# Last attention unit: P·V in 32-row pieces, with probabilities transposed in place by VectorE

## Chip, cores, metric

The kernel runs on one core of one Trainium2 chip, in one launch. The time is the device time of an execution in microseconds. Before the change it is 1957.69 us, the median of 3 runs (1957.03 to 1958.97).

## What is computed

One layer of a hybrid trunk for a prompt of 1024 tokens and 8 samples of 16 tokens, all in fp32, with weights shared: RMS norm, one large input projection, attention in chunks of 64 frames that see themselves and 8 chunks back, a Mamba-2 scan (SSD) with a causal convolution ahead of it, gates, and an output projection. The change touches only the attention over the prompt, of which this is the core:

```python
def attend(q, k, v, bias, mask):
    s = jnp.einsum('bqhd,bkhd->bhqk', q, k).astype(jnp.float32) * (ATT_HEAD_DIM ** -0.5) + bias[None].astype(jnp.float32)
    s = jnp.where(mask, s, -1e30)
    p = jax.nn.softmax(s, axis=-1).astype(v.dtype)
    return jnp.einsum('bhqk,bkhd->bqhd', p, v)
```

There are 16 heads of 64 channels. The last line, probabilities times V, is what is done in another way, and for the last two heads only.

## The kernel before

**Dense work.** Most of TensorE's time goes to the projections (`dense`, L442, L443, L445; `dense_tok`, L506 to L508): each fp32 product is three fp32r matmuls of 128x128 weights on 384 tokens (high by high, high by low, low by high). The halves of the weights are made by a copy on ScalarE (L334) and a subtraction on VectorE (L335) after a load (L312). A dense result lies in a PSUM bank, `d` (two of them) or `s` (one, shared with the attention scores), until an eviction reads it.

**Attention units.** Eight units, u = 0 to 7, hold two heads each. `prompt()` of a unit goes through 8 blocks of 128 queries, m = 0 to 7, in the four score rounds of the table `ROUNDS` and a last one. A round first transposes the probabilities of the blocks in its third column (`transposed`, L1043: TensorE transposes of 128x128 into a `g` bank, copied back to SBUF on ScalarE at L1045 or VectorE at L1047), then forms P·V of the blocks in its second column (`weigh`, L1066, evicted with the gate at L1127), then the scores of its first column (L1122, into the `s` bank and two `g` banks). After the scores VectorE forms the negated row minimum (`negated`, L1036), ScalarE the exponential (L1031), VectorE the reciprocal and the scale (L1032, L1033). There are four `g` banks. `weigh` uses one of them at a time, the two heads on the two halves of the array's columns: 64 columns of weights each (V) and 128 moving columns. In unit 7 its three calls come to 12, 18 and 30 matmuls of the program, of two passes each, as fp32 takes two.

**What surrounds unit 7.** It is the last attention unit, and its V is ready early: the last token block is projected 45 us before its first P·V. Next comes the SSD part, in head pairs p. Pair 0 first projects its gate `z` (evictions `evz`, L1423 on ScalarE and L1424 on VectorE), then runs its convolution (`conv_gen`: ScalarE L1260, L1265, VectorE L1263 three times, L1269, L1270), and its prelude loads the decay sums `acs_d` to all partitions (L1441) and runs nine ScalarE steps on them (L1453) and an exponential (L1457). The sums come from `dt_gen` (L1291 to L1342). `sample()` (L1152 on) is the samples' attention.

**Order.** A planner on the host runs these parts as generators. It sets their order by a clock of its own (`until`, `pause`, `yield` of a cost), and a scheduler below it places the instructions of each engine by its own estimate, with `late` keeping program order. Each engine then runs its list in order, and waits at the head of it. A generator that finds no slot in SBUF for a buffer is held (`walloc`). The area `varena` (6144 columns) becomes `va_ssd` after unit 7's last token projection (`v_phase("ssd", F32)`), where the layout `L_VT` has five slots `T` of 1184 columns, which `alloc` tries first for the SSD's `T` buffers, `z` among them.

Of the kernel before, what the change touches and what calls it, by code (L numbers as in the profile page):

```python
# [121 lines left out]
def trunk_kernel(ctx: ExitStack, tc: tile.TileContext, h):  # L122
# [41 lines left out]
    def pg(cols=512):  # L164
        return psg.tile([P, 512], F32, tag="g", name=nm("g"))[:, :cols]
# [58 lines left out]
    L_QS = qarena.set_layout(0, [("ada", 1, 1024)])  # L224
    L_VA = varena.set_layout(0, [("ada", 6, 1024)])
    L_VT = varena.set_layout(0, [("T", 5, 1184)])
    v_open = [False]

    def alloc(lay, tag, cols, cold=None):
        if lay is L_Q:  # L230
            try:
                return alloc(L_QR, tag, cols)
            except NoSlot:
                pass
        if lay is L_SSD and tag == "H":
            try:
                return Buf(qarena, qarena.alloc(L_QS, "ada", cols), cols)
            except NoSlot:
                pass
        if lay is L_Q or lay is L_QS:  # L240
            return Buf(qarena, qarena.alloc(lay, tag, cols), cols)
        if lay is L_W3 or lay is L_W7 or lay is L_VT or lay is L_VA:
            return Buf(varena, varena.alloc(lay, tag, cols), cols)
        if lay is L_H or lay is L_W or lay is L_WA or lay is L_QR or lay is L_ST:
            return Buf(rarena, rarena.alloc(lay, tag, cols, cold), cols)
        if (lay is L_SSD or lay is L_HEAD or lay is L_TAIL) and tag == "T" or lay is L_HEAD and tag == "Y":
            if v_open[0]:
                try:
                    return alloc(L_VT, "T", cols)
                except NoSlot:  # L250
                    pass
        return Buf(arena, arena.alloc(lay, tag, cols), cols)
# [659 lines left out]
    def attention(u):  # L912
# [4 lines left out]
        def dense_gen():  # L917
            qk = yield from walloc(lay, "Q", 16 * P)
            v = yield from walloc(lay, big, NT)
            nb = yield from walloc(lay, "n", 84)  # L920
            st["qk"], st["v"], st["nb"] = qk, v, nb
            if u == NU - 1:
                dts["raw"] = yield from walloc(lay, "T", NT)

            def ev(t, ps):

                while t == 8 and "turned" not in st:
                    blocked[0] = "q and k of the first tokens"
                    yield None
                c = qk.ap[:, 2 * (t % 8) * P:2 * (t % 8 + 1) * P]  # L930
                nc.scalar.activation(c, ps[:, :2 * P], AF.Copy)
                s = alloc(lay, "q", 2 * P)
                nc.scalar.activation(s.ap, ps[:, :2 * P], AF.Square)
                nc.vector.tensor_copy(v.ap[:, t * P:(t + 1) * P], ps[:, 2 * P:NQ])
                if u == NU - 1:
                    nc.vector.tensor_copy(dts["raw"].ap[:, t * 32:(t + 1) * 32], ps[:, NQ:])
                nc.vector.tensor_reduce(nb.ap[:, 4 * t:4 * t + 4], s.ap.rearrange("p (h d) -> p h d", d=HD), mybir.AxisListType.X, ALU.add)
                s.free()
                st["n"] = t + 1

            yield from dense_tok(ev)
            dma(h["out_v"][u], v.ap[:, 512:])
            if u == NU - 1:
                v_phase("ssd", F32)
                v_open[0] = True
                return
            z = zs[u + 1] = yield from walloc(lay, "Z" if u + 1 == NU - 1 else "T", NT)
            yield from dense(hops, ev_z(z))
# [72 lines left out]
        def done():  # L1021
            st["left"] -= 1
            att_left[0] -= 1
            if st["left"] == 0:
                dma(att_d[u], st["z"].ap)
                for n in ("z", "v"):
                    st[n].free()
# [21 lines left out]
        def prompt():  # L1049
# [7 lines left out]
            def weigh(js, po):  # L1057
# [16 lines left out]

            ROUNDS = (
# [6 lines left out]
            for pieces, js, ts in ROUNDS:  # L1084
                yield from until(max([sfree[0]] + [tpt[j] for j in js if j in tpt]))
                for m in ts:
                    n = min(m, 4) + 1
                    for e in range(2):
                        yield from until(probs[m] + 700 * e)
                        x, at = place[m][e]  # L1090
                        transposed(x.ap[:, at:at + n * P], x.ap[:, at:at + n * P], n)
                        yield 109 * n
                    tpt[m] = clock[0] + 1500

                yield from until(max([clock[0] + 1000] + [tpt[j] for j in js]) if ts else 0.0)
                cost, po = 0, None
                if js:
                    po = pg(len(js) * P)
                    cost += weigh(js, po)
                for m in sorted({x[0] for x in pieces}):  # L1100
# [21 lines left out]
                            late(nc.tensor.matmul(banks[k][e][:, o:o + w], x.r[hs, qs], y.r[hs, kk], start=i == 0, stop=i == 2))  # L1122
                    cost += 3 * (max(w, 240) / 2.27 + 10)
                yield cost
                if js:
                    ms = slice(js[0] * P, (js[-1] + 1) * P)
                    nc.vector.scalar_tensor_tensor(z.ap[:, ms], po, 0.5, z.ap[:, ms], ALU.mult, ALU.mult)  # L1127
                t = clock[0] + 1000
                for m, c, w, k, o in pieces:
# [8 lines left out]
                    if c + w == n * P:  # L1138
# [7 lines left out]
                        if m == 7:  # L1146
                            for x in st["ops"] + bias:
                                x.free()
                sfree[0] = clock[0] + 300 + sum(3.2 * x[2] for x in pieces)
            done()  # L1150

        def sample():  # L1152
# [772 lines left out]
```

## Time and profile before

| | |
|---|---|
| time, median of 3 runs | 1957.69 us |
| span of the profiled execution | 1955.7 us |
| PE busy | 1938.3 us (99%), 14091 matmuls |
| DVE busy | 1168.5 us (60%) |
| ACT busy | 776.4 us (40%) |
| granted TensorE clock | full in all 40 slices |
| unit 7: scores of the last round on PE | 716.5 to 717.9 us |
| unit 7: last P·V on PE | 735.1 to 738.2 us |

The profiled execution has no time of its own beside its span; the median of the runs stands 2.0 us above that. A group of the profile is a line with an engine, an operation, its tiles and shapes, its count, its busy time, the mean of one instruction in ns, and the idle time before them with what ended it. TensorE's matmuls overlap, so the mean of one (275 ns) is no price; the distance from start to start is. Each matmul has a weight load (PEld) that is counted apart.

### The profile page before, as it was taken

How to read it: one execution, taken by the hardware profiler on the slowest of the kernel's cores; microseconds unless marked ns; L12 is line 12 of the kernel's file. 1: busy time of each engine (PE TensorE's matmuls, PEld its weight loads, DVE VectorE, ACT ScalarE, POOL GpSimd, SP SyncE). 2: the span in 40 equal slices, each digit the busy share in tenths (PEclk: the TensorE clock that was granted, in tenths of full speed). 3: DMA queues.
4: the chain of work that ended last, by engine and by line, in shares of the span. 5: the costliest groups of instructions: out<-in, count | busy, mean ns of one | idle time of the engine just before them, and what ended most of it. 6: DMA issues, size and time to landing. Idle time of an engine off the chain costs nothing.

```text
span 1955.7 us, 35068 instructions
## 1 busy us (share of the span) xinstructions
PE 1938.3 (99%) x14091; PEld 1859.4 (95%) x14091; DVE 1168.5 (60%) x2441; ACT 776.4 (40%) x1589; POOL 323.5 (17%) x624
## 2 busy tenths in 40 slices
PE   7999999999999999999999999999999999999999
PEld 5999999899998999999999999999999999999999
DVE  7455555556555765757566666576674334777732
ACT  8444444445444557344454434345351301111200
POOL 0312213122131201212212221122212100000000
PEclk9999999999999999999999999999999999999999
DMA  9124244232432325433333333332337642331241
GB/s 367 60 81 131 86 132 131 90 122 88 131 112 96 112 88 160 128 112 110 95 132 129 106 103 114 117 118 91 117 118 291 234 140 92 104 104 56 86 143 52
DMA packets 81209, 238.62 MB, mean 122 GB/s; under 512 B 14284, under 2 KB 15320, under 8 KB 81048
## 3 DMA queue, kind: packets, MB, share of 16 engines
q1 hardware_dynamic: 72088, 207.74, 32.7%
q0 software_dynamic: 8960, 28.65, 3.8%
q8 instruction: 111, 1.82, 0.4%
q14 instruction: 50, 0.41, 0.1%
HBM read 192.70 MB, written 43.66 MB: 121 GB/s over the span
## 4 chain that ended last, share of the span: by engine, by line
PE 96%; DVE 1%; ACT 1%; DMA 1%; issue 0%; SPq 0%
PE d L442 13%; PE d L443 13%; PE d L445 13%; PE s L442 5%; PE s L445 5%; PE s L443 5%; PE d L508 5%; PE d L506 5%; PE d L507 5%; PE g L1043 3%; PE g L1066 3%; PE g L1553 2%; PE s L1122 2%; PE g L1526 1%; PE g L1573 1%; PE g L1122 1%
## 5 line engine op out<-in xcount | busy, mean ns | idle before, releaser
L442 PE MATMUL d<-rarena 128*128 128x384 f32 x1520 | 517.4, 340 | 0.3 <-ACT arena L1355 0.3
L445 PE MATMUL d<-rarena 128*128 128x384 f32 x1520 | 511.4, 336 | 0.0
L443 PE MATMUL d<-rarena 128*128 128x384 f32 x1520 | 511.0, 336 | 0.0
L442 PEld LDWEIGHTS d<-rarena 128*128 128x128 f32 x1520 | 285.6, 188 | 4.6 <-issue 2.3
L443 PEld LDWEIGHTS d<-rarena 128*128 128x128 f32 x1520 | 285.6, 188 | 2.8 <-issue 2.4
L445 PEld LDWEIGHTS d<-rarena 128*128 128x128 f32 x1520 | 285.5, 188 | 1.1 <-issue 0.9
L334 ACT ACTIVATE rarena<-arena 128x1024 fp32r<-128x1024 f32 x92 | 97.5, 1060 | 314.1 <-PE s L443 226.2
L442 PE MATMUL s<-rarena 128*128 128x384 f32 x640 | 216.7, 339 | 0.0
L443 PE MATMUL s<-rarena 128*128 128x384 f32 x640 | 214.2, 335 | 0.0
L445 PE MATMUL s<-rarena 128*128 128x384 f32 x640 | 214.1, 334 | 0.0
L508 PE MATMUL d<-va_att,rarena 128*128 128x384 f32 (+1 forms) x559 | 195.0, 349 | 0.0
L506 PE MATMUL d<-va_att,rarena 128*128 128x384 f32 (+1 forms) x559 | 193.9, 347 | 0.0
L507 PE MATMUL d<-va_att,rarena 128*128 128x384 f32 (+1 forms) x559 | 191.0, 342 | 0.0
L335 DVE TENSOR_TENSOR rarena<-arena,rarena 128x1024 fp32r<-128x1024 f32 x92 | 113.2, 1230 | 82.7 <-ACT rarena L334 82.4
L1031 ACT ACTIVATE arena<-arena 128x640 f32<-128x640 f32 (+2 forms) x144 | 101.4, 706 | 138.0 <-DVE arena L1140 99.7
L442 PEld LDWEIGHTS s<-rarena 128*128 128x128 f32 x640 | 120.3, 188 | 1.0 <-issue 1.0
L443 PEld LDWEIGHTS s<-rarena 128*128 128x128 f32 x640 | 120.3, 188 | 0.0
L445 PEld LDWEIGHTS s<-rarena 128*128 128x128 f32 x640 | 120.1, 188 | 0.0
L508 PEld LDWEIGHTS d<-va_att,rarena 128*128 128x128 f32 x559 | 105.5, 189 | 3.9 <-issue 2.7
L1263 DVE SCALAR_TENSOR_TENSOR arena<-arena 128x1176 f32<-128x1176 f32 x66 | 99.9, 1514 | 15.5 <-ACT arena L1260 14.2
L506 PEld LDWEIGHTS d<-va_att,rarena 128*128 128x128 f32 x559 | 105.2, 188 | 3.1 <-issue 1.2
L507 PEld LDWEIGHTS d<-va_att,rarena 128*128 128x128 f32 x559 | 105.2, 188 | 1.0 <-issue 0.4
(345 smaller groups left out, 3212.9 us busy)
## 6 DMA issues: line engine op xcount, KB each, us to landing
arena<-in_wall_dram SPq DMA_DIRECT2D x85, 512.0 KB, 3.9
arena<-in_kc_dram SPq DMA_DIRECT2D x64, 256.0 KB, 4.2
arena<-in_vc_dram SPq DMA_DIRECT2D x64, 256.0 KB, 3.4
arena<-acs_d SPq DMA_DIRECT2D x19, 576.0 KB, 3.8
gate_d<-arena POOLq DMA_DIRECT2D x48, 192.0 KB, 2.5
arena<-y_d SPq DMA_DIRECT2D x15, 576.0 KB, 5.6
arena<-in_wssd_dram SPq DMA_DIRECT2D x16, 512.0 KB, 4.1
arena<-in_wada_dram SPq DMA_DIRECT2D x15, 512.0 KB, 8.9
```

Source lines behind the costliest of these rows:

```text
L334: keep(nc.scalar.activation(hi.r[:, c], b.ap, AF.Copy))
L335: keep(nc.vector.tensor_tensor(lo.r[:, c], b.ap, hi.ap[:, c], ALU.subtract))
L442: nc.tensor.matmul(ps, hi.r[:, wc], kh.r[:, tok], start=k == 0, stop=False)
L443: nc.tensor.matmul(ps, hi.r[:, wc], kl.r[:, tok], start=False, stop=False)
L445: nc.tensor.matmul(ps, lo.r[:, wc], kh.r[:, tok], start=False, stop=k == nk - 1)
L506: nc.tensor.matmul(ps, kh.r[:, tok], wh, start=j == 0, stop=False)
L507: nc.tensor.matmul(ps, kh.r[:, tok], wl, start=False, stop=False)
L508: nc.tensor.matmul(ps, kl.r[:, tok], wh, start=False, stop=j == KT - 1)
L1031: nc.scalar.activation(p, p, AF.Exp, bias=sm_[:, 4 + e:5 + e], scale=-1.0, accum_out=sm_[:, 6 + e:7 + e])
L1043: nc.tensor.transpose(ps[:, s * P:(s + 1) * P], p[:, (j + s) * P:(j + s + 1) * P], ident)
L1122: late(nc.tensor.matmul(banks[k][e][:, o:o + w], x.r[hs, qs], y.r[hs, kk], start=i == 0, stop=i == 2))
L1263: nc.vector.scalar_tensor_tensor(yc, r.ap[:, j:j + n], w4[:, i, j:j + 1], yc, ALU.mult, ALU.add)
```

## The change

For unit 7 alone ("rows" in its state), P·V is cut along the keys into blocks of 32. (1) After V is projected, 16 DMAs copy it inside SBUF into a buffer `vr` of 4096 columns, so that every group of 32 partitions holds all keys' V; `vr` lies in `va_ssd` and is freed when `prompt()` of unit 7 is done. 4096 columns lie over the first four of the five `T` slots. (2) The transposes on TensorE and the copies after them go; `turn` transposes each probability buffer in place on VectorE, in blocks of 32x32 (16 instructions, two for each of the eight m). (3) `weigh_rows` replaces `weigh`. For a block of 32 keys and one or two m it issues 8 matmuls with 32 rows and 64 columns of weights: four row groups (32 queries each), by two column groups (the heads), the moving side 64 or 32 columns. Each row group writes a `g` bank of its own, so it holds all four. Its three calls have 20, 20 and 44 blocks, so 84, or 672 matmuls of the program and 1344 of the profile. (4) Four evictions per call, one for each bank, in place of one. (5) `prompt()` of unit 7 waits for the copies (12 us by the planner's clock), and its P·V now comes ahead of the round's scores with pauses of its own.

```diff
--- before.py
+++ after.py
@@ -224,6 +224,7 @@
     L_QS = qarena.set_layout(0, [("ada", 1, 1024)])
     L_VA = varena.set_layout(0, [("ada", 6, 1024)])
     L_VT = varena.set_layout(0, [("T", 5, 1184)])
+    L_VR = varena.set_layout(0, [("r", 1, 32 * P)])
     v_open = [False]
 
     def alloc(lay, tag, cols, cold=None):
@@ -239,7 +240,7 @@
                 pass
         if lay is L_Q or lay is L_QS:
             return Buf(qarena, qarena.alloc(lay, tag, cols), cols)
-        if lay is L_W3 or lay is L_W7 or lay is L_VT or lay is L_VA:
+        if lay is L_W3 or lay is L_W7 or lay is L_VT or lay is L_VR or lay is L_VA:
             return Buf(varena, varena.alloc(lay, tag, cols), cols)
         if lay is L_H or lay is L_W or lay is L_WA or lay is L_QR or lay is L_ST:
             return Buf(rarena, rarena.alloc(lay, tag, cols, cold), cols)
@@ -942,6 +943,13 @@
             dma(h["out_v"][u], v.ap[:, 512:])
             if u == NU - 1:
                 v_phase("ssd", F32)
+                vr = alloc(L_VR, "r", 32 * P)
+                r4 = vr.ap.rearrange("p (t j c) -> p t j c", j=4, c=P)
+                v3 = v.ap[:, :NP].rearrange("p (t c) -> p t c", c=P)
+                for j in range(4):
+                    for i in range(4):
+                        dma(r4[32 * i:32 * i + 32, :, j], v3[32 * j:32 * j + 32])
+                st["rows"] = vr, clock[0] + 12000
                 v_open[0] = True
                 return
             z = zs[u + 1] = yield from walloc(lay, "Z" if u + 1 == NU - 1 else "T", NT)
@@ -1074,6 +1082,56 @@
 
 
 
+            def turn(m, e):
+                n = min(m, 4) + 1
+                x, at = place[m][e]
+                nc.vector.transpose(x.ap[:, at:at + n * P], x.ap[:, at:at + n * P])
+
+            def weigh_rows(js):
+
+                vr = st["rows"][0].ap
+                pq = [pg(32 * len(js)) for _ in range(4)]
+                first_kb = lambda m: 4 * max(m - 4, 0)
+                ops = []
+                for a in range(0, len(js), 2):
+                    ms = js[a:a + 2]
+                    common = range(first_kb(ms[-1]), 4 * ms[0] + 4)
+                    ops += [(kb, a, ms) for kb in common]
+                    if len(ms) == 2:
+                        ops += [(kb, a, ms[:1]) for kb in range(first_kb(ms[0]), first_kb(ms[1]))]
+                        ops += [(kb, a + 1, ms[1:]) for kb in range(4 * ms[0] + 4, 4 * ms[1] + 4)]
+                begun, left = set(), {a: sum(o[1] <= a < o[1] + len(o[2]) for o in ops) for a in range(len(js))}
+                for kb, a, ms in ops:
+                    begin = a not in begun
+                    for i in range(len(ms)):
+                        assert begin == (a + i not in begun)
+                        begun.add(a + i)
+                        left[a + i] -= 1
+                    end = left[a] == 0 or left[a + len(ms) - 1] == 0
+                    for i in range(4):
+                        rw = slice(32 * i, 32 * i + 32)
+                        for e in range(2):
+                            at = [place[m][e][0].at + place[m][e][1] + 32 * (kb - first_kb(m)) for m in ms]
+                            if len(at) == 1:
+                                mv = arena.base[rw, at[0]:at[0] + 32]
+                            else:
+                                d = at[1] - at[0]
+                                lo = min(at)
+                                mv = arena.base[rw, lo:lo + 2 * abs(d)].rearrange("p (a c) -> p a c", a=2)[:, :, :32]
+                                if d < 0:
+                                    mv = mv[:, ::-1]
+                            he = slice(64 * e, 64 * e + 64)
+                            out = pq[i][he, 32 * a:32 * (a + len(ms))]
+                            if len(ms) > 1:
+                                out = out.rearrange("p (a c) -> p a c", c=32)
+                            late(nc.tensor.matmul(out, vr[rw, kb * P + 64 * e:kb * P + 64 * e + 64], mv, start=begin, stop=end,
+                                                  skip_group_check=True))
+                for j in js:
+                    for x, _ in place.pop(j):
+                        if not any(x is y for q in place.values() for y, _ in q):
+                            x.free()
+                return pq, len(ops) * 16 * 6.7
+
             ROUNDS = (
                 (((0, 0, 128, 0, 0), (2, 0, 384, 0, 128), (1, 0, 256, 1, 0), (3, 0, 256, 1, 256)), (), ()),
                 (((3, 256, 256, 0, 0), (4, 0, 256, 0, 256), (4, 256, 384, 1, 0), (5, 0, 128, 1, 384)), (), (0, 1, 2)),
@@ -1088,13 +1146,24 @@
                     for e in range(2):
                         yield from until(probs[m] + 700 * e)
                         x, at = place[m][e]
+                        if "rows" in st:
+                            turn(m, e)
+                            continue
                         transposed(x.ap[:, at:at + n * P], x.ap[:, at:at + n * P], n)
                         yield 109 * n
                     tpt[m] = clock[0] + 1500
 
                 yield from until(max([clock[0] + 1000] + [tpt[j] for j in js]) if ts else 0.0)
                 cost, po = 0, None
-                if js:
+                if js and "rows" in st:
+                    yield from until(max([st["rows"][1]] + [clock[0] + 2500] if ts else [0.0]))
+                    pq, c = weigh_rows(js)
+                    yield c
+                    zv = z.ap[:, js[0] * P:(js[-1] + 1) * P].rearrange("p (a q c) -> p q a c", q=4, c=32)
+                    for i in range(4):
+                        nc.vector.scalar_tensor_tensor(zv[:, i], pq[i].rearrange("p (a c) -> p a c", c=32), 0.5, zv[:, i], ALU.mult, ALU.mult)
+                    yield from pause(1500)
+                elif js:
                     po = pg(len(js) * P)
                     cost += weigh(js, po)
                 for m in sorted({x[0] for x in pieces}):
@@ -1122,7 +1191,7 @@
                             late(nc.tensor.matmul(banks[k][e][:, o:o + w], x.r[hs, qs], y.r[hs, kk], start=i == 0, stop=i == 2))
                     cost += 3 * (max(w, 240) / 2.27 + 10)
                 yield cost
-                if js:
+                if js and po is not None:
                     ms = slice(js[0] * P, (js[-1] + 1) * P)
                     nc.vector.scalar_tensor_tensor(z.ap[:, ms], po, 0.5, z.ap[:, ms], ALU.mult, ALU.mult)
                 t = clock[0] + 1000
@@ -1147,6 +1216,8 @@
                             for x in st["ops"] + bias:
                                 x.free()
                 sfree[0] = clock[0] + 300 + sum(3.2 * x[2] for x in pieces)
+            if "rows" in st:
+                st["rows"][0].free()
             done()
 
         def sample():
```

How the lists of the engines change shows at three places. Names: `s_`, `g_`, `d_` with a number are PSUM buffers, numbered in the planner's order; line numbers after the change are those of the changed kernel.

TensorE before, at the end of the last round's scores (`g_7549`, `g_7550` are the score banks; `d_7788` and `d_7869` are projections, the first of them `z` of the first SSD pair):

```order
L1122 MATMUL g_7549<-rarena 128x256
L1122 MATMUL g_7550<-rarena 128x256
L1327 MATMUL g_7607<-va_ssd,arena 128x256
L443 MATMUL d_7788<-rarena 128x384
L1335 MATMUL g_7613<-arena 32x128 x4
L445 MATMUL d_7788<-rarena 128x384
L442 MATMUL d_7869<-rarena 128x384
```

Seventy-four more projection matmuls stand between these scores and the last P·V, with the transposes of blocks 6 and 7 among them. The same place after the change (`g_7906` is the first of the four banks of the last P·V, `s_8374` the third part of `z`):

```order
L1191 MATMUL g_7862<-rarena 128x256
L1191 MATMUL g_7863<-rarena 128x256
L1127 MATMUL g_7906<-arena,va_ssd 64x64
L443 MATMUL s_8374<-rarena 128x384
L444 MATMUL s_8374<-rarena 128x384
```

The first matmul of the last P·V now follows the scores directly, then come 24 projection matmuls into the `s` bank, and then the rest of P·V. The earlier P·V calls moved as well: counted in projection matmuls, from 662 after a fixed point to 648 (first call) and from 716 to 696 (second), where the last scores went from 718 to 696.

TensorE before, at the end of the last P·V:

```order
L445 MATMUL s_7947<-rarena 128x384
L1066 MATMUL g_7728<-arena 64x128 x30
L1335 MATMUL g_7777<-arena 32x128
L1202 MATMUL g_7798<-arena 32x128 x20
L442 MATMUL d_7977<-rarena 128x384
```

After the change (`g_7906` to `g_7909` are its four banks):

```order
L1127 MATMUL g_7906<-arena,va_ssd 64x32 x2
L1127 MATMUL g_7907<-arena,va_ssd 64x32 x2
L1127 MATMUL g_7908<-arena,va_ssd 64x32 x2
L1127 MATMUL g_7909<-arena,va_ssd 64x32 x2
L443 MATMUL d_8437<-rarena 128x384
```

`d_8437` is the next projection. All of `z` (`d_8267`, `d_8311`, `s_8374`) now stands ahead of the end of P·V, and it fills both `d` banks and the `s` bank.

ScalarE before, around its last exponentials of unit 7 (L1031), where `z` was evicted already (`d_7788`):

```order
L1423 ACTIVATE va_ssd<-d_7788 128x384
L1336 ACTIVATE va_ssd<-g_7624 32x512
L1045 ACTIVATE arena<-g_7639 128x512
L1031 ACTIVATE arena<-arena 128x640 x2
L1045 ACTIVATE arena<-g_7658 128x512
L1240 ACTIVATE arena<-d_7869 128x384
```

After the change (L1039 is that exponential, L335 the weights' copy, L1524 and L1528 the prelude's steps, L1331 the convolution, L1494 the evictions of `z`):

```order
L1039 ACTIVATE arena<-arena 128x640 x2
L335 ACTIVATE rarena<-arena 128x1024
L1524 ACTIVATE arena<-arena 128x128 x9
L1528 ACTIVATE arena<-arena 128x1152
L1331 ACTIVATE va_ssd<-arena 128x1176
L1494 ACTIVATE va_ssd<-d_8267 128x384
L1336 ACTIVATE arena<-va_ssd 128x1176
L1494 ACTIVATE va_ssd<-d_8311 128x384
L1494 ACTIVATE va_ssd<-s_8374 128x384
```

The evictions of `z` come behind the prelude's nine steps, which need the load of `acs_d`, and behind a convolution step. On VectorE the second half of the eviction of `d_8267` (L1495) comes behind two of that convolution's steps (L1334). On SP's queue the load of `acs_d` (L1512) stands behind two loads of weights (L313), which wait for VectorE's halves (L336).

## Prediction

> **What bounds the kernel now.** I read the head of the page first, then what TensorE waited for.
>
> ```profile
> span 1955.7 us, 35068 instructions
> PE 1938.3 (99%) x14091; PEld 1859.4 (95%) x14091; DVE 1168.5 (60%) x2441; ACT 776.4 (40%) x1589; POOL 323.5 (17%) x624
> ```
>
> ```profile
> PE g L577 <- DMA arena<-in_xT_dram: 8.7, 1, 8.7
> ...
> PE g L1481 <- DVE arena L1269: 1.8, 2, 1.4
> ...
> PE g L1043 <- DVE arena L1036: 0.4, 2, 0.3
> ```
>
> TensorE is busy 99% of the span, and of its idle time 8.7 us are the start. So a microsecond of matmuls saved is a microsecond gained, no wait of VectorE or ScalarE costs anything today, and each wait that the change opens on TensorE costs in full. That leaves two questions: how many microseconds of matmuls go or come, and whether the projections still cover the chain scores, softmax, P·V.
>
> **The matmuls that go and come.** First the groups, then the timeline and the chain for what one instruction really takes (start to start, not its mean).
>
> ```profile
> L1043 PE MATMUL g<-arena 128*128 128x128 f32 x560 | 86.2, 274 | 0.4 <-DVE arena L1036 0.4
> L1066 PE MATMUL g<-arena 128*64 128x128 f32 x960 | 57.7, 275 | 0.0
> ```
>
> ```profile
> 691.72 1.58 PE L1043 MATMUL g<-arena 128*128 128x128 f32 x13
> 693.06 0.42 PE L445 MATMUL d<-rarena 128*128 128x384 f32 x1
> ```
>
> ```profile
> 735.18 3.43 PE g L1066 x60
> ...
> 903.72 0.89 PE g L1560 x32
> ```
>
> 13 transposes run from 691.72 to the next start at 693.06, 0.103 us each; 60 go, 6.2 us. P·V takes 3.43/60 = 0.057 us for each instruction; unit 7's 60 matmuls are 120 instructions, 6.9 us. Added are 84 blocks of 8 matmuls in two passes, 1344 instructions. The nearest row is L1560: 64 columns of weights and 16 moving, two column groups side by side: 0.89/32 = 0.028 us for each, so 0.056 us for a pass of one group. If all eight tiles of a block (four row groups, two column groups) run side by side as these two do, a block is two passes, 0.112 us, and 84 blocks are 9.4 us. If the row groups follow one another, a block is 0.45 us and the sum 37.6 us. For which of the two, the timeline has rows. The first is an answer for a window of 0.027 us:
>
> ```profile
> 657.02 0.32 PE L1202 MATMUL g<-arena 128*32 128x128 f32 x4
> ```
>
> ```profile
> 689.81 0.33 PE L442 MATMUL d<-rarena 128*128 128x384 f32 x1
> 689.98 0.33 PE L443 MATMUL d<-rarena 128*128 128x384 f32 x1
> ...
> 717.49 0.28 PE L1122 MATMUL g<-rarena 64*128 64x256 f32 x2
> 717.60 0.28 PE L1122 MATMUL g<-qa_att,rarena 64*128 64x256 f32 x2
> ```
>
> Four column groups start within 0.027 us, and the two row groups of the scores take 0.11 us a pair with 256 columns, where one projection with 384 takes 0.17, so 256 would take 0.115: a pair costs what one does. Column groups and row groups each run side by side here; that all eight do is an inference. I take 9.4 us, with 37.6 as the upper end; the matmuls then change by 9.4 - 6.2 - 6.9 = -3.7 us.
>
> The Trainium skill ("TensorE: Matmul & The Clock Gate", section "Wait — 56ns, not 53.3ns?") says that matmuls never start closer together than about 25 ns, however few columns move. By it the estimate would be 1344 x 25 ns = 33.6 us in place of 9.4. The four starts within 27 ns speak against it for tiles side by side, but the average of 28 ns over 32 doesn't; it is part of rival one.
>
> **The copies** of V (16 DMAs) have the 45 us between V and its first use, with SP nearly empty: nothing, or a late first P·V.
>
> **The waits that come.** The order shows the new chain: `z` fills both `d` banks and the `s` bank ahead of the last P·V and can't be evicted, so TensorE has no projection to put beside the softmax. Durations:
>
> ```profile
> L335 DVE TENSOR_TENSOR rarena<-arena,rarena 128x1024 fp32r<-128x1024 f32 x92 | 113.2, 1230 | 82.7 <-ACT rarena L334 82.4
> L1263 DVE SCALAR_TENSOR_TENSOR arena<-arena 128x1176 f32<-128x1176 f32 x66 | 99.9, 1514 | 15.5 <-ACT arena L1260 14.2 <-POOL arena L1252 0.7
> L1033 DVE TENSOR_SCALAR arena<-arena 128x640 f32<-128x640 f32 x80 | 51.7, 648 | 2.7
> L1535 DVE SCALAR_TENSOR_TENSOR arena<-arena,g 128x64 f32<-128x64 f32 x224 | 45.9, 274 | 57.4 <-ACT arena L1531 53.1 <-PE g L1526 4.3
> ...
> L1032 DVE RECIPROCAL arena<-arena 128x1 f32<-128x1 f32 x144 | 23.1, 161 | 44.6 <-ACT arena L1031 42.8
> ...
> L1036 DVE CUSTOM_DVE_ANT_0 arena<-s,arena 128x640 f32<-128x640 f32 x16 | 13.1, 821 | 3.7 <-PE s L1178 3.7
> ...
> L1424 DVE SCALAR_TENSOR_TENSOR va_ssd<-va_ssd,d 128x384 f32<-128x384 f32 x21 | 11.5, 546 | 2.5 <-ACT va_ssd L1423 2.5
> ...
> L1036 DVE CUSTOM_DVE_ANT_0 arena<-s,arena 128x512 f32<-128x512 f32 x16 | 10.4, 688 | 2.3 <-PE s L1122 2.3
> ```
>
> ```profile
> L1031 ACT ACTIVATE arena<-arena 128x640 f32<-128x640 f32 x80 | 65.9, 824 | 119.0 <-DVE arena L1140 95.5 <-DVE arena L1036 23.5
> ...
> L1260 ACT ACTIVATE arena<-arena 128x1176 f32<-128x1176 f32 x22 | 30.1, 1370 | 0.6 <-DVE arena L1270 0.2
> ...
> L1031 ACT ACTIVATION_READ_ACCUMULATOR arena<-arena 128x1 f32 x144 | 27.2, 189 | 0.0
> ...
> L1457 ACT ACTIVATE arena<-arena 128x1152 f32<-128x1152 f32 x19 | 22.0, 1160 | 0.2
> ```
>
> ```profile
> 717.69 0.29 DVE L1036 CUSTOM_DVE_ANT_0 arena<-s,arena 128x128 f32<-128x128 f32 x1 [0.79 <-PE s L1122]
> ...
> 718.24 0.16 DVE L1140 TENSOR_TENSOR arena<-arena 128x2 f32<-128x2 f32 x1
> ...
> 722.44 0.42 DVE L1036 CUSTOM_DVE_ANT_0 arena<-g,arena 128x256 f32<-128x256 f32 x1
> ...
> 722.78 0.42 DVE L1036 CUSTOM_DVE_ANT_0 arena<-g,arena 128x256 f32<-128x256 f32 x1
> ```
>
> The last two start 0.34 us apart for a duration of 0.42: in a row, VectorE's instructions cost 0.08 less than they last, and so I count them. The in-place transpose of 640 columns has no row; between the plain pass (0.65) and the pass with a minimum (0.82) I take 0.7. In place of 4 of TensorE's transposes and two copies it now stands on VectorE itself, in the chain.
>
> A, the second P·V needs all four `g` banks. From the end of the first P·V VectorE has to do 4 evictions (0.8), the samples' minimum (0.7), wait for their exponential (0.82 + 0.19), reciprocal and scale (0.7): 3.3 us. ScalarE's convolution step ends at 4.0, the three L1263 at 8.3, two minima of 512 at 9.5, L1140 and the exponential at 10.7, reciprocals and a scale at 11.6, the transpose at 12.3, a scale at 12.9, and the two minima that free the `g` banks at 14.1. TensorE in this time has 31 projection matmuls at 0.173 (5.4), 0.5 of L1335's transposes, and the scores:
>
> ```profile
> 698.06 0.50 PE L1122 MATMUL s<-rarena 64*128 64x512 f32 x2
> ...
> 699.66 0.44 PE L445 MATMUL d<-rarena 128*128 128x384 f32 x1
> ```
>
> 1.6 us, in all 7.5. A is 6.6 us.
>
> B, the first matmul of the last P·V stands directly behind the scores and needs the transposed block 6. From VectorE's first minimum (before, 0.24 us ahead of the scores' end): minima 0.55, L1140, exponential, reciprocal, scale, reciprocal to 2.6, transpose to 3.3: TensorE waits 3.1. `s_8374` needs the `s` bank read: a scale and two minima of 384, 1.4 more. B is 4.5 us. Its 24 matmuls last to 9.0, and the remaining 44 blocks, whose transposes are ready in time (the last at 11.6), to 13.9.
>
> C, `d_8437` needs a `d` bank, so the eviction of `d_8267`.
>
> ```profile
> 762.08 2.74 ACT va_ssd L1453 x9
> ...
> 769.83 4.62 DMA arena<-acs_d
> ```
>
> VectorE finishes the weights' half (L335) at 13.0, behind which SP issues the load of `acs_d`: landed at 17.7. ScalarE's nine steps end at 20.4, the exponential at 21.6, the convolution step at 22.9; two L1263 on VectorE end at 25.8, and L1424 at 26.3. C is 26.3 - 13.9 = 12.4 us. At least it is 1 us (the eviction alone), if the load lands early.
>
> D, the work behind `d_8437` waits for the other evictions, 0 to 2 us: 1.
>
> The waits come to 24.5 us, with 11 to 28 as bounds. Of the waits before, L1043's 0.4 goes and L1481's 1.8 may: -1.
>
> **The clock after a wait.** Two windows at the start, for L577 alone (time busy and count on PE, then on PEld):
>
> ```profile
> 9.67:13.94 4.27, 4.27 (x6) 1.60 (x5) 1.00 1.02 420
> 15.05:17.20 2.15, 2.15 (x6) 0.95 (x5) 1.00 0.98 330
> ```
>
> Five loaded weights, so five matmuls, take 4.27 us after the first idle time and 2.15 us later, twice as fast, though the granted clock reads 1.00 in both. From 8.7 to about 14.4 us TensorE ran at half speed, which loses some 2.7 us. Waits as long as A and C may each bring that back: 0 to 5.4 us; I take 4, since A is the shorter.
>
> By the Trainium skill ("TensorE: Matmul & The Clock Gate", section "What's actually happening") an idle window of about 3.4 us halves the clock until a busy one of the same length, an estimate of 1.7 us lost for each of A and C, 3.4 in place of 4. The start agrees in kind; no longer wait stands in this trace.
>
> The sum: -3.7 + 24.5 - 1 + 4 = +23.8 us, against the span 1955.7, so 1979.5. The runs' median stands 2.0 above the span (1957.69), so 1981.5 us.
>
> **Rivals.** One: the eight tiles don't run side by side, or no instruction comes closer than 28 ns on average; both give 37.6 us in place of 9.4, +28.2. The last P·V then ends at 9.0 + 19.7 = 28.7, behind C's chain, so C falls to 1, and its half-speed stretch goes: 23.8 + 28.2 - 11.4 - 2 = +38.6, 1996 us (by the skill's 25 ns about 1992). For it: no row has eight tiles at once. Against it: rows for both kinds of group.
>
> Two, the other side: TensorE doesn't wait, because the projections cover the chain as they did before, and only the matmuls count: -3.7 - 0.4, 1953.6 us. Its place is the stretch from the first P·V to `d_8437`; it decides once the waits together are under 4 us. For it: 24 of `z`'s matmuls do move into the softmax of block 7, and VectorE is busy 60%. Against it: A needs the 14.1 us chain of VectorE to shrink to 8, and the three banks are held.
>
> Three: the load of `acs_d` lands early, A and B shrink by half, no half speed: 5.5 + 1 + 1 - 4.7 = +3, 1960.5 us.
>
> **How the numbers follow.** The forecast has 0.72, with a range of its own of 1968 (C at 6, clock 0, smaller A) to 1991 (clock 5.4, D 2, a block at 0.2 us, which adds 7.4); rival one 0.13, two 0.09, three 0.06. A measurement of this kernel tells 0.2% (3.9 us) from no change. Faster by more: rival two, 0.09. Within: rival three, 0.06. Slower: 0.85. The range of 8 in 10 reaches down to 1965, leaving out rivals two and three, and up to 1997, to take in rival one.
>
> **What would show it.** Right: TensorE waits of about 6.6 us before the second P·V, 3 and 1.4 around the last one's first matmul, and 12 before `d_8437`, named after VectorE's minima, the transpose and the eviction; 84 blocks in about 10 us outside the waits; half-speed projections for some us behind the long waits. Wrong: blocks of 0.4 us (rival one); TensorE busy 99% with `z` evicted before the prelude's steps (two); the load of `acs_d` landed before the last P·V ends (three).

## The result, and the profile after

The changed kernel takes 1994.45 us, the median of 4 runs (1992.66 to 1996.03), against 1957.36: a ratio of 1.0188, 95% interval 1.0176 to 1.02. It was forecast slower at 1981.5, within 1965 to 1997. The loss is 37 us where 24 were expected, and of another make.

The head of the page after, and the queue that brings the engines their instructions:

```profile
span 1992.8 us, 37402 instructions
PE 1954.8 (98%) x15255; PEld 1872.1 (94%) x15255; DVE 1174.2 (59%) x2456; ACT 767.9 (39%) x1571; POOL 325.6 (16%) x624
...
q8 instruction: 120, 1.97, 0.4%
```

The same queue before:

```profile
q8 instruction: 111, 1.82, 0.4%
```

The span grew by 37.1 us, TensorE's busy time by 16.5 and its idle time by 20.6. What it waited for after the change, in the view of waits (total, times, longest):

```profile
PE g L1127 <- issue: 14.0, 8, 2.2
...
PE g L1127 <- DVE arena L1044: 3.3, 1, 3.3
PE g L1127 <- DVE arena L1088: 3.0, 1, 3.0
...
PE s L443 <- DVE arena L1044: 0.9, 1, 0.9
PE g L1127 <- ACT va_ssd L1407: 0.5, 1, 0.5
```

Four of these lines were forecast: A is 3.3 + 0.5, B is 3.0 + 0.9. The largest was not. "issue" is time in which the engine waited for nothing that the profile shows, and all of it lies inside P·V (L1127). TensorE's timeline shows where:

```profile
741.89 2.26 PE L1127 MATMUL g<-arena,va_ssd 32*64 32x64 f32 x188
746.35 1.73 PE L1127 MATMUL g<-arena,va_ssd 32*64 32x64 f32 x128 [2.20 <-issue]
750.08 2.06 PE L1127 MATMUL g<-arena,va_ssd 32*64 32x32 f32 x128 [2.00 <-issue]
753.81 2.03 PE L1127 MATMUL g<-arena,va_ssd 32*64 32x32 f32 x128 [1.67 <-issue]
757.26 2.04 PE L1127 MATMUL g<-arena,va_ssd 32*64 32x32 f32 x128 [1.42 <-issue]
761.01 0.32 PE L1127 MATMUL g<-arena,va_ssd 32*64 32x32 f32 x2 [1.70 <-issue]
761.25 0.69 PE L443 MATMUL d<-rarena 128*128 128x384 f32 x1
```

Behind the first stretch of 188 matmuls, P·V comes in portions of exactly 128, each with its weight load, so 256 instructions, with a gap behind each. From one portion's start to the next are 3.73 us twice (746.35, 750.08, 753.81), then 3.45 and 3.75; over the four that is 3.67, or 29 ns a matmul. The changed kernel has 15255 - 14091 = 1164 more matmuls, 2328 instructions with their loads, or 9.1 portions of 256, and the instruction queue carried 120 - 111 = 9 more packets, of 16 KB each (1.97 MB / 120). So a portion is one packet of instructions. The trace has the packets' own times, and they agree: between 741.8 and 761.5 us there are 5 packets for the 5 gaps above. They end at 745.09, 748.74, 752.54, 755.88 and 759.47, each 1.3 to 1.5 us before a portion starts, and from the second on each begins 1.0 to 1.2 us after the portion before it has started. So in these rows the next portion hangs on the packet before it, and the packet on the start of the portion before that.

TensorE's time can be added up by line, from each matmul's start to the next one's. P·V in pieces takes 39.6 us, with the gaps and with the 3.3 and 0.9 us of waits that lie inside it. P·V in the old way takes 7.0 us less than before and the transposes 6.5 less. The projections take 4.9 us more, the scores 3.8 more (B's 3.0 among them), the samples' scores 1.5 more. That makes 36.3 of the 37.1.

Apart from the waits of A and B, the projections and scores are dearer because of the clock. Windows of the changed kernel (PE busy and count, then the granted clock):

```profile
700.00:705.00 5.00, 2.89 (x297) 1.00 0.02 3
705.00:710.00 5.00, 5.00 (x47) 0.66 0.02 3
...
720.00:725.00 5.00, 3.59 (x239) 0.50 0.03 7
735.00:740.00 5.00, 5.00 (x16) 0.50 0.30 105
765.00:770.00 5.00, 5.00 (x49) 1.00 0.59 147
```

Between 735 and 740 us 16 projection matmuls take 0.31 us each in place of 0.17. The mean granted clock is 0.989 over the span, which makes 44 us at half clock, all in this stretch.

### The profile page after: what moved, and what is told of

The parts are those of the page before. It is cut to its first block, busy times and chain, and to the rows that moved or that the text cites. A ratio compares the mean times of both kernels' runs of the same rounds, so it can differ in the third digit from the quotient of the medians.

```text
span 1992.8 us, 37402 instructions
## 1 busy us (share of the span) xinstructions
PE 1954.8 (98%) x15255; PEld 1872.1 (94%) x15255; DVE 1174.2 (59%) x2456; ACT 767.9 (39%) x1571; POOL 325.6 (16%) x624
## 3 DMA queue, kind: packets, MB, share of 16 engines
q8 instruction: 120, 1.97, 0.4%
## 4 chain that ended last, share of the span: by engine, by line
PE 94%; DVE 2%; DMA 2%; ACT 1%; issue 1%; SPq 0%; DVEq 0%; ACTq 0%
PE d L443 13%; PE d L444 13%; PE d L446 13%; PE s L443 5%; PE s L444 5%; PE s L446 5%; PE d L509 5%; PE d L507 5%; PE d L508 5%; PE g L1051 3%; PE g L1074 2%; PE g L1624 2%; PE s L1191 2%; PE g L1597 1%; PE g L1191 1%; PE g L1644 1%
## 5 line engine op out<-in xcount | busy, mean ns | idle before, releaser
L443 PE MATMUL s<-rarena 128*128 128x384 f32 x648 | 220.8, 341 | 0.9 <-DVE arena L1044 0.9
L335 ACT ACTIVATE rarena<-arena 128x1024 fp32r<-128x1024 f32 x93 | 98.4, 1058 | 312.9 <-PE s L444 227.2
L444 PE MATMUL s<-rarena 128*128 128x384 f32 x648 | 218.1, 337 | 0.0
L446 PE MATMUL s<-rarena 128*128 128x384 f32 x648 | 217.8, 336 | 0.0
L1039 ACT ACTIVATE arena<-arena 128x640 f32<-128x640 f32 (+2 forms) x144 | 101.5, 706 | 165.9 <-DVE arena L1209 119.4
L336 DVE TENSOR_TENSOR rarena<-arena,rarena 128x1024 fp32r<-128x1024 f32 x93 | 114.2, 1228 | 63.7 <-ACT rarena L335 63.4
L443 PEld LDWEIGHTS s<-rarena 128*128 128x128 f32 x648 | 122.6, 189 | 2.1 <-DVE arena L1044 1.0
L444 PEld LDWEIGHTS s<-rarena 128*128 128x128 f32 x648 | 122.7, 189 | 0.2 <-issue 0.2
L446 PEld LDWEIGHTS s<-rarena 128*128 128x128 f32 x648 | 122.5, 189 | 0.0
L1334 DVE SCALAR_TENSOR_TENSOR arena<-arena 128x1176 f32<-128x1176 f32 x69 | 106.4, 1542 | 16.1 <-ACT arena L1331 15.2
```

Source lines behind the costliest of these rows:

```text
L335: keep(nc.scalar.activation(hi.r[:, c], b.ap, AF.Copy))
L336: keep(nc.vector.tensor_tensor(lo.r[:, c], b.ap, hi.ap[:, c], ALU.subtract))
L443: nc.tensor.matmul(ps, hi.r[:, wc], kh.r[:, tok], start=k == 0, stop=False)
L444: nc.tensor.matmul(ps, hi.r[:, wc], kl.r[:, tok], start=False, stop=False)
L446: nc.tensor.matmul(ps, lo.r[:, wc], kh.r[:, tok], start=False, stop=k == nk - 1)
L1039: nc.scalar.activation(p, p, AF.Exp, bias=sm_[:, 4 + e:5 + e], scale=-1.0, accum_out=sm_[:, 6 + e:7 + e])
```

## Experiments

Two theories after the result. **S (supply):** TensorE's instructions arrive no faster than 256 in 3.7 us, so P·V costs what its number of instructions costs, whatever the array does with them. **R (array):** a block takes the array its time, and the gaps are a fixed cost. Beside them stands the prediction's own reason for the waits, **H (held slots)**, against **O**, that the turn on VectorE moves P·V ahead of the projections.

**Parts of the change alone.** The copies of V with their slots, without turn and pieces:

```diff
-                        if "rows" in st:
+                        if False:
                             turn(m, e)
...
-                if js and "rows" in st:
+                if js and False:
```

> V is copied to the row groups and the copies hold their place among the T slots until unit 7 is done, but the transposes on TensorE and the old P.V stay, so the output is the reference's. Theory H (held slots, the prediction's reason for the waits): z has no slot, projections are missing beside the softmax, and waits of 8 us or more come: 1965 to 1977 us. Theory O (order: the waits come with the turn on VectorE, which costs TensorE nothing, so that P.V moves ahead of the projections): the old order stands, 74 or more projection matmuls remain between the last scores and the last P.V, 1957 us within 4.

1954.4 us (10 runs), ratio 0.9986 (0.9976 to 0.9995): as O has it, and slightly faster than before (0.14%). Its complete list of waits on TensorE:

```profile
PE g L578 <- DMA arena<-in_xT_dram: 7.8, 1, 7.8
PE s L666 <- ACT rarena L647: 0.9, 1, 0.9
PE s L666 <- DVE rarena L659: 0.9, 1, 0.9
PE d L694 <- DVE arena L685: 0.4, 1, 0.4
PE g L1552 <- DVE va_ssd L1340: 0.2, 1, 0.2
```

Of the 1.8 + 0.4 + 0.3 us that TensorE waited before in the middle of the kernel, 0.2 is left, which is most of the 2.8 us gained. With the next run it is the fastest kernel of this study; nobody reads the copies in it, so the gain must be one of order.

The turn alone:

```diff
-                vr = alloc(L_VR, "r", 32 * P)
...
-                        if "rows" in st:
+                        if u == NU - 1:
                             turn(m, e)
```

> The probabilities are turned on VectorE in 32x32 blocks, with no copies of V and no held slots, and the old P.V of 128 rows reads them (a block transpose is not the transpose, so the attention of unit 7 is wrong). Theory H: only the transposes go, 6.5 us, and nothing waits: 1951 us. Theory O: 6.5 us go, waits of 3 to 8 us before the second and the last P.V come, and some us at half clock after them: 1957 to 1964 us.

1954.75 us, ratio 0.9988 (0.9979 to 0.9997): between the two. TensorE waits in three new places, 2.5 + 0.9 + 0.7 us, and the transposes' 6.5 us pay for it. Of the 74 projection matmuls between the last scores and the last P·V 19 are left: the turn does move P·V ahead, as O has it.

Turn and copies, with the old P·V:

```diff
-                if js and "rows" in st:
+                if js and False:
```

> Turn on VectorE and copies of V with their held slots, but the old P.V of 128 rows (unit 7's attention is wrong). Theory H: 8 us or more above the run with the turn alone. Theory O: within 3 us of that run, and the changed kernel stands some 30 us above this one, all of it from the P.V in 32-row pieces.

1960.05 us, ratio 1.0012 (1.0002 to 1.0021), 5.3 above the turn alone: neither 3 nor 8. One wait makes most of it, on the timeline:

```profile
718.02 0.48 PE L1051 MATMUL g<-arena 128*128 128x128 f32 x1 [7.09 <-ACT arena L1053]
```

So without the pieces the change costs about 3 us (0.4 to 4.1 by the interval). The pieces cost 1994.45 - 1960.05 = 34.4 us. Neither theory has the 5.3 us: held slots alone cost nothing (the first run), but beside the turn they do, though nobody reads the copies here. How, these runs don't show.

**What the pieces cost.** Four row groups made one, the blocks kept:

```diff
-                    for i in range(4):
-                        rw = slice(32 * i, 32 * i + 32)
+                    for i in range(4) if begin or end else (kb % 4,):
+                        rw = slice(32 * i, 32 * i + 32) if begin or end else slice(0, P)
```

> The changed kernel, but in all blocks except the first and the last of an output one matmul of 128 rows stands in place of the four of 32 (so P.V sums over the wrong rows): 246 matmuls of the program in place of 672, 492 instructions in place of 1344, with the same 84 blocks, columns, banks and order. Theory S (supply: TensorE's instructions arrive at about 29 ns a matmul once they follow each other so closely, 128 in a burst and then a gap): 852 x 0.029 = 25 us less, 1970 us, and less than that by some us if the clock stays up; the gaps of 1.4 to 2.2 us are gone. Theory R (the array takes 0.16 to 0.25 us for a block, whatever it is made of): only the 14 us of gaps go, 1980 us or more.

1982.0 us, ratio 1.0125 (1.011 to 1.014). By the time alone that is R's range. But the gaps are gone, and P·V without its waits falls from 35.4 to 16.2 us, 19 us less, where R allows 14 and S wants 25. That the time falls by 12.5 only has another reason, to be seen in TensorE's rows:

```profile
733.20 6.21 PE L1127 MATMUL g<-arena,va_ssd 32*64 32x64 f32 x234
...
745.42 1.33 PE L1051 MATMUL g<-arena 128*128 128x128 f32 x5 [6.01 <-DVE arena L1164]
747.73 0.69 PE L443 MATMUL d<-rarena 128*128 128x384 f32 x1 [0.98 <-DVE va_ssd L1495]
```

With P·V over at 739.4, the evictions of `z` and of P·V are late: 7 us of waits come back that the slow P·V had hidden.

Each matmul of P·V twice:

```diff
-                            late(nc.tensor.matmul(out, ..., start=begin, stop=end, skip_group_check=True))
+                            for again in range(2):
+                                late(nc.tensor.matmul(out, ..., start=begin and again == 0, stop=end and again == 1, ...))
```

> The changed kernel with each of the 672 matmuls of P.V issued twice in a row, 1344 more instructions (so its sums are doubled). Theory S (supply): 1344 x 0.029 = 39 us more, 2033 us, with the gaps after each 128 matmuls more than doubled in number. Theory R (the array's own time, 10 to 15 ns a matmul inside a burst, and a fixed number of waits): 13 to 20 us more, 2008 to 2014 us.

2031.3 us (2 runs), ratio 1.0378 (1.0357 to 1.0399): 36.8 us more, S. The portions:

```profile
777.76 2.76 PE L1128 MATMUL g<-arena,va_ssd 32*64 32x32 f32 x128 [1.00 <-issue]
781.49 2.73 PE L1128 MATMUL g<-arena,va_ssd 32*64 32x32 f32 x128 [0.97 <-issue]
785.22 2.73 PE L1128 MATMUL g<-arena,va_ssd 32*64 32x32 f32 x128 [1.00 <-issue]
```

A portion is busy for 2.7 us here and 2.0 in the changed kernel, the gap is 1.0 and not 1.4 to 2.0, and the distance is 3.73 again. Most distances of the two runs lie near it, all between 3.45 and 4.56. It is the distance that stays, and not the gap.

Twice the moving columns:

```diff
-                pq = [pg(32 * len(js)) for _ in range(4)]
+                pq = [pg(64 * len(js)) for _ in range(4)]
...
+                            mv = mv.unsqueeze(1).to_broadcast([32, 2] + list(mv.shape[1:]))
```

> The changed kernel with each matmul's moving columns taken twice (128 or 64 in place of 64 or 32, the second half into columns that nobody reads): the same 1344 instructions, twice the array's moving time. Theory S: the array's time hides in the gaps of the supply, 1994.5 us within 4. Theory R: 168 passes become 0.05 us longer at full clock and 0.1 at half, 8 to 17 us more, 2003 to 2011 us.

1993.0 us, ratio 1.0183 (1.0168 to 1.0199): S; the array's added time went into the gaps (11.4 us of them in place of 14.0), and P·V without its waits takes 36.2 us against 35.4.

One head in most blocks:

```diff
                         for e in range(2):
+                            if e and not (begin or end):
+                                continue
```

> The changed kernel without the second head's matmuls, except in the first and last block of an output (so the second head's P.V is mostly left out): 776 instructions in place of 1344, the same blocks, banks and order. Theory S: 568 x 0.029 = 16.5 us less, of which up to 6 come back as a wait behind the last P.V (as where four row groups were made one): 1978 to 1984 us. Theory R: the two heads stand side by side in the array, so a block takes as long without one; only gaps in proportion go, 14 x 0.42 = 6 us: 1988 us or more.

1983.0 us, ratio 1.0134 (1.0117 to 1.015): in S's range. Where P·V ended, the forecast's wait C stands:

```profile
742.62 2.02 PE L1129 MATMUL g<-arena,va_ssd 32*64 32x32 f32 x74 [2.14 <-issue]
750.47 0.69 PE L443 MATMUL d<-rarena 128*128 128x384 f32 x1 [5.83 <-DVE va_ssd L1497]
```

The pieces with TensorE's transposes:

```diff
-                        if "rows" in st:
+                        if False:
                             turn(m, e)
```

> The changed kernel, but with the transposes on TensorE as before (so P.V in 32-row pieces reads wrongly ordered probabilities). The order has no projections between the last scores and the last P.V here either. Theory: the pieces carry nearly the whole loss, and the turn on VectorE saves them 60 transposes and shortens the chain: 6.5 us and 2 to 6 us of waits more than the changed kernel, 2003 to 2007 us. Rival: the turn is what makes the pieces dear (it fills VectorE and takes the projections away): then this run lies 10 us or more below the changed kernel, 1984 us or less.

1994.6 us, ratio 1.0191 (1.0176 to 1.0206), the changed kernel's time. Neither side of the expectation: the turn doesn't make the pieces dear, but it doesn't save them 6.5 us either. By line, the transposes take 10.7 us more than in the changed kernel, waits of 3.0 us included, P·V 4.4 less, since A and B are not there, and the projections 5.2 less. The slots are held in this kernel, so held slots and pieces without the turn don't make A and B.

**Held slots and the place of the instructions.** No copies, V read where it lies:

```diff
-                vr = alloc(L_VR, "r", 32 * P)
...
-                st["rows"] = vr, clock[0] + 12000
+                st["rows"] = v, clock[0] + 12000
...
-    vr[rw, kb * P + 64 * e:kb * P + 64 * e + 64]
+    vr[rw, kb // 4 * P + 64 * e:kb // 4 * P + 64 * e + 64]
```

> The changed kernel without the copies: the pieces read V where it lies (so keys and V don't belong together), nothing lies in z's slots, and no eviction of z waits for the last P.V. In the runs with copies but without pieces nobody read the copies, so z's evictions had nothing to wait for, and held slots were not tried there. Theory H (held slots take the projections away): the order has 94 projection matmuls between the last scores' start and the last P.V again; the waits before the second and the last P.V go (3.3 + 0.5 + 3.0 + 0.9 us) and some 3 us of projections at half clock with them: 1984 us. Rival: the waits belong to the turn or to the four banks: 1994 us within 3.

1981.0 us, ratio 1.0129 (1.0113 to 1.0144): H, by 3 us more than expected. In TensorE's list of waits A and B are gone, and in P·V only the supply is left:

```profile
PE g L1121 <- issue: 12.4, 7, 2.2
```

The same kernel with projections between the blocks (a lock keeps the planner's other parts out meanwhile):

```diff
+                    if len(done_) % 2:
+                        yield 214
+                        yield from pause(200)
...
-                    pq, c = weigh_rows(js)
+                    lock[0] = cur[0]
+                    pq, c = yield from weigh_rows(js)
```

> The run without the copies, with P.V in the same 1344 instructions but three projection matmuls after every second block. Theory S (supply): two blocks and three projections are 70 instructions in about 1.06 us, so 256 in 3.9 us, about what the supply gives; the gaps go, a block costs 0.27 us (0.15 for its passes, the rest for changing between tiles and the whole array), 84 of them 23 us in place of 35: 1967 us. Rival: P.V costs what its instructions take wherever they stand, and each change adds: 1984 us or more.

1976.4 us, ratio 1.0103 (1.0088 to 1.0118): between the two, 4.6 below the run before it. Two blocks and what stands around them:

```profile
745.43 0.49 PE L1126 MATMUL g<-arena 32*64 32x64 f32 x32
745.85 0.44 PE L443 MATMUL d<-rarena 128*128 128x384 f32 x1
746.13 0.34 PE L444 MATMUL d<-rarena 128*128 128x384 f32 x1
746.30 0.33 PE L446 MATMUL d<-rarena 128*128 128x384 f32 x1
746.57 0.49 PE L1126 MATMUL g<-arena 32*64 32x64 f32 x32
```

For P·V S has it: no gaps between these blocks, 32 matmuls in 0.42 us to the next projection, and P·V's whole time down from 31.6 to 21.7 us (some of it still stands in two long portions, with 4.0 us of gaps). What was not expected is the price around it: three projections take 0.72 us from 745.85 to 746.57 in place of 0.52, so each change to the tiles and back costs 0.2. Only the last P·V call came out spread, with 22 such changes, 4.4 us in all; the projections take 4.1 us more than in the run before.

No copies, and one matmul of 128 rows for four of 32:

```diff
-                    for i in range(4):
-                        rw = slice(32 * i, 32 * i + 32)
+                    for i in range(4) if begin or end else (kb % 4,):
+                        rw = slice(32 * i, 32 * i + 32) if begin or end else slice(0, P)
...
-                st["rows"] = vr, clock[0] + 12000
+                st["rows"] = v, clock[0] + 12000
```

> The run without the copies, with one matmul of 128 rows in place of four of 32 in all blocks but the first and the last of an output (P.V sums over the wrong rows), 492 instructions. Theory: with neither held slots nor more instructions than the supply gives, what is left is 1957.4 - 13.5 for the matmuls removed + 492 x 0.025 = 12.3, 1956 us. Rival: the waits behind P.V that this kernel with the copies showed (6 us) stay: 1962 us or more.

1965.5 us, ratio 1.0049 (1.0032 to 1.0066): 9 above the theory and in the rival's range, but not with the rival's 6 us of waits. P·V took 14.4 us against the 13.5 saved, so the pieces would not have gained even at 492 instructions. In the profiled execution, with a span of 1960.2, a wait of 3.3 us stands behind P·V; what the other runs spent beyond that is open.

## The prediction, step by step

- **What bounds it: right.** With TensorE at 99%, every added matmul and wait was paid.
- **Matmuls removed:** 13.1 us forecast, 13.5 measured.
- **Blocks: the step that failed.** "84 blocks are 9.4 us" became 39.6 less the waits inside (4.2), 35.4 us. That tiles run side by side was right: in the spread run the eight matmuls of a pass start within 0.05 us, and 32 take 0.42 us to the next projection, 13 ns each; the fastest portion of the changed kernel is through in 1.73 us, 13.5 ns a matmul. But a rate per instruction from a run of 32 says nothing of 1344: behind the first portion they come at 29 ns. Rival one named this number ("no instruction comes closer than 28 ns on average"), with its time, 1996, and 0.13; it is the case that came, by another mechanism than tiles one after another.
- **A:** 6.6 forecast, 3.8 measured. VectorE's chain was right: 14.1 us forecast, 13.8 measured from its first eviction at 705.24 to TensorE's start at 719.03. TensorE had 10.0 us to do meanwhile and not 7.5, mostly since its projections ran at half clock for some of it.
- **B:** 4.5 forecast, 3.9 measured, at the place and behind the instructions named.
- **C:** 12.4 forecast, none measured. Its chain came as written, only later, and P·V was slower still. On VectorE and ScalarE after the change:

```profile
730.08 0.29 DVE L1044 CUSTOM_DVE_ANT_0 arena<-s,arena 128x128 f32<-128x128 f32 x1 [1.45 <-PE s L1191]
...
756.34 2.92 DVE L1334 SCALAR_TENSOR_TENSOR va_ssd<-arena,va_ssd 128x1176 f32<-128x1176 f32 x2 [4.68 <-ACT va_ssd L1331]
759.18 0.55 DVE L1495 SCALAR_TENSOR_TENSOR va_ssd<-va_ssd,d 128x384 f32<-128x384 f32 x1
```

```profile
751.12 2.74 ACT L1524 ACTIVATE arena<-arena 128x128 f32<-128x128 f32 x9 [8.23 <-DMA arena<-acs_d]
```

  The eviction ends 29.6 us after VectorE's first minimum (26.3 forecast), when P·V, due at 13.9, still has until 31. Rival one had C fall to 1. Where P·V was shortened, C came back with 5.8 us, so it was hidden and not wrong, though no run shows its 12.4.
- **D and the waits of before:** D, 1 us forecast, is not in the list of waits. Of the 0.4 and 1.8 us before, 1.6 are left (L1552), 0.6 less where 1 was taken.
- **Reason for the waits: half right.** With pieces and turn present and nothing held, A and B went, as H has it. They also went with the slots held and the transposes on TensorE, and held slots alone made no wait. So A and B need the held slots and the turn together; how the held slots bring them about is not shown.
- **Clock:** 4 us forecast for two long waits. Measured are 4.4 us on projections (4.9 less A's 0.5) and 0.8 on scores, with the clock at half for 44 us, and not only behind long waits: it first fell between 705 and 710 us, behind the first P·V and before A. The Trainium skill ("TensorE: Matmul & The Clock Gate", section "What's actually happening") asks for an idle window of about 3.4 us; here P·V with gaps of at most 2.2 us (2.1 in the first call) was enough, so the rule was too mild for this stream.

The sum with the sizes measured, -13.5 + 35.4 + 3.8 + 3.9 + 5.2 - 0.6 = 34.2, leaves 2.9 of the 37.1. 1.5 of it are the samples' scores, for a reason that I did not find.

That the time lies in the forecast's range is in part luck. The blocks cost 26.0 us more than forecast and the four waits 16.8 less (7.7 for 24.5), and the two errors cancel in good part. The forecast's own range ended at 1991; only the stretch up to 1997, taken in for rival one, holds the measured time.

The Trainium skill's floor of about 25 ns between starts (the same page, section "Wait — 56ns, not 53.3ns?") does not hold for the tiles here: the fastest portion has 13.5 ns a matmul. By it the forecast would have come nearer all the same (1992), since the limit that acts, on long streams, lies at 29.

## What to carry to other kernels

Count instructions when a change cuts work into small pieces, not only array time: a price per matmul read from a run of 32 doesn't hold for a run of several hundred. Read from the trace whether a gap or a distance is fixed; work that is doubled and costs nothing (the columns), beside work that costs its number (the matmuls), tells supply from array. A long wait that doesn't come may only be hidden behind another loss, so shorten that one before calling the wait wrong.

## What the hardware showed

- TensorE's stream of small matmuls is delivered in portions of 128 with their weight loads, one packet of 16 KB each. When they are run faster than they come, the portions start 3.45 to 4.56 us apart, mostly 3.73, while the array works through 128 in 1.73 to 2.06 us.
- Eight tiles of 32x64 do run side by side: the eight of a pass start within 0.05 us, and 32 matmuls, two blocks, take 0.42 us to the next projection.
- A change between the whole array and tiles costs about 0.2 us there and back.
- The granted clock fell to half behind the first P·V, whose gap was 2.1 us, before any longer wait.
- VectorE's transpose of 128x640 in 32x32 blocks, which the trace before didn't show, takes 0.83 us; to the next instruction's start it is 0.74 (732.67 to 733.41), where 0.7 was assumed:

```profile
732.67 0.83 DVE L1088 STREAM_TRANSPOSE arena<-arena 128x640 f32<-128x640 f32 x1
```
